# One stage of a delta-rule layer, rescheduled: mask product, convolution taps, key scaling, scores and output transposes

## The chip, the core and the metric

The kernel runs on one core of a Trainium2 chip. Its engines are TensorE (PE; its weight loads are a row of their own, PEld), VectorE (DVE), ScalarE (ACT), GpSimd (POOL) and SyncE (SP), which only issues DMAs here. The metric is the device time of one execution in microseconds (us); less is better.

## The reference, cut to what matters

One layer: a gated DeltaNet with eight heads beside a memory cross-attention, an output projection, and a SwiGLU feed-forward part. The change touches the DeltaNet alone. What it computes for each head:

```python
qkv = silu(causal_dwconv(qkv, conv_w))          # 4 taps along time
q = l2norm(q) * GDN_DK ** -0.5;  k = l2norm(k)
beta = sigmoid(b);  g = -exp(a_log) * softplus(a + dt_bias);  G = cumsum(g) in a chunk
decay = where(incl, exp(G_i - G_j), 0)
lower = where(strict, beta_i * (k_i . k_j) * decay, 0)
sol = triangular_solve(lower + I, [v * beta, k * beta * exp(G)])     # u, w
p = (q k^T) * decay;  qg = q * exp(G);  kg = k * exp(G_last - G)
# over chunks: v_new = u - w S;  o = qg S + p v_new;  S = S * exp(G_last) + kg^T v_new
y = rms_norm(o, out_norm) * silu(z)
```

The kernel uses chunks of 128 rows, which gives the same result.

## The kernel before

**Units and slots.** A head has eight chunks. Half a head (four chunks, `C4`, 128 x 512 elements) is a unit; there are 16 units, and the loop over `i` runs through 20 rounds. In round `i` four things go on side by side: the dense projection that makes the inputs of the heads (`dense`: 512-column matmuls of fp32r operands that are split into a high part `whi`, `uhi` and a low part `wlo`, `ulo`, three per product), the preparation of unit `i`, the inverse of unit `i-1` (`inverse`), and the recurrence over the four chunks of unit `i-2` (`scan`). Each round has 16 slots. In a slot stand one step of the inverse, one step of the scan, the steps that the table `STEPS` lists for that slot (function, lag in units), then perhaps one convolution tap (`TAPS`), then two groups of three dense matmuls (one group where a round has a single projection). An even round projects v and q of a head, an odd round k of the next head and z.

**The recurrence.** In the scan a chunk takes four slots: `r` (slots 0, 4, 8, 12), `vn` (1, 5, 9, 13), the new state `st` (2, 6, 10, 14), the output `po` (3, 7, 11, 15). TensorE makes a product into PSUM, VectorE turns it into the operand of the next product. The matmul `pc<-vn,kg` of slots 2, 6, 10 and 14 needs the `vn` of the slot before. The inverse goes on in the same way: even slots `pz`, then `zlev` on VectorE; odd slots `pT` and `pU`, then `T` and `U` on VectorE. Each of these takes the result of the slot before.

**What sets the order.** On TensorE the order is that of the code (`keep_in_program_order`, rounds 2 to 15). On the other engines a scheduler places the instructions; `tc.issue_after(x)` keeps an instruction behind `x`. `crit[0]` is the last VectorE instruction of inverse or scan so far; `tap()` puts its tap behind it. Each engine then works strictly through its own order.

**The steps that the change touches.** `conv_silu` leaves for each projected half two ScalarE copies from PSUM (`cb` L289, `cv` L290) and three taps on VectorE (L295, each reads `cb` and `cv` from SBUF); after the third, ScalarE applies Silu (L298). Halves end with slots 3, 7, 11 and 15. `k_norm` transposes the keys (`pk`), copies them to SBUF (`kh`, L435) and makes the inverse norm `rk` (squares on ScalarE, power on GpSimd, L85). `k_scale` multiplies `kh` by `rk` on VectorE (L443). `k_decay` makes `kg` (L449, two SBUF inputs) and on GpSimd `E` (L454, L455). `k_system` makes the matrix `at`, its fp16 high part `ah` (ScalarE, L485) and low part `al` (GpSimd, L486). `k_pairs` multiplies `ah` by a mask into `U` (L491, fp16, both inputs in SBUF); `k_first` transposes that `U` in slot 15 (`ptt`, `T` L499). `q_scores` makes `pqk`, `E` (L572) and `gr` (L573, GpSimd). `post` scales the output on GpSimd (L624 to L630), `post_y` transposes it (`pyt`) and multiplies it by z (L635), then stores it. Beside this GpSimd makes the low part of each weight tile, `wlo` (L93, 128 x 1024), and in odd rounds four differences of output weights, `wsum` (L650).

```python
    STEPS = {0: ((post, -3), (k_decay, 0)), 2: ((k_turn, 0),), 4: ((v_turn, -1),), 5: ((q_turn, -1),),
             7: ((k_system, 0),), 9: ((post_y, -3),), 10: ((k_norm, 1),), 11: ((q_scores, -1),), 13: ((k_pairs, 0),),
             15: ((k_scale, 1),)}
    TAPS = (0, 1, 2, 4, 5, 6, 8, 10, 11, 12, 14, 15)
```

Of the kernel before, what the change touches and what calls it, by code (L numbers as in the profile page):

```python
# [13 lines left out]
AF = mybir.ActivationFunctionType  # L14
ALU = mybir.AluOpType
AX = mybir.AxisListType

P = 128
# [36 lines left out]
def trunk_kernel(ctx: ExitStack, tc: tile.TileContext, a: dict, out: bass.AP):  # L55
    nc = tc.nc
# [122 lines left out]
    for tn in range(NT):  # L179
        hf, n = divmod(tn, 4)  # L180
# [22 lines left out]
        for q in range(2):  # L203
            pt = bank(("ms", "iv")[q], "pt")
            for j in range(4):
# [6 lines left out]
                                    in1=hi.bitcast(F32), op=ALU.subtract)  # L212
# [12 lines left out]
    C4 = 4  # L225
# [9 lines left out]
    mu = load_const(a["mu"], [P, P], F16, "mu_sb", up)  # L235
# [32 lines left out]
    def u4(tag, bufs, dt=F32, name=None):  # L268
        return hp.tile([P, C4, P], dt, tag=tag, name=name or tag, bufs=bufs)

    def flat(t):
        return t.rearrange("p n c -> p (n c)")
# [4 lines left out]
    def bc(col):  # L277
        return col.unsqueeze(2).broadcast_to([P, C4, P])
# [26 lines left out]
    def tap():  # L305

        while pending:
            with tc.issue_after(crit[0]) if crit[0] is not None else nullcontext():
                if next(pending[0], 0) is None:
                    return  # L310
            pending.pop(0)
# [3 lines left out]
            tap()  # L315

    crit = [None]

    def transposes(src, name):
        pt = bank("ms", name)  # L320
# [36 lines left out]
    st = [{} for _ in range(2 * H)]  # L357
# [23 lines left out]
    def tmp(name):  # L381
        return xp.tile(shp, F32, tag=name, name=name, bufs=1)

    beta, neg_eg, eg_last, eg_tot, gc = ct("beta"), ct("neg_eg"), ct("eg_last"), ct("eg_tot"), ct("gc")
# [35 lines left out]
                            in1=gc.rearrange("p h n -> p (h n)"), op=ALU.subtract)  # L420
# [10 lines left out]

    def k_norm(h, hf, hd, st):
        pk = transposes(hd["kT"][:, hf * C4:(hf + 1) * C4, :], "pk")
        kh = u4("kh", 2)
        nc.scalar.copy(flat(kh), pk)  # L435
        rk = small.tile([P, C4], F32, tag="rk", name="rk")
        rstd_into(rk, sumsq(pk), 1.0, C4)
        st.update(kh=kh, rk=rk)

    def k_scale(h, hf, hd, st):  # L440
        kh = st["kh"]
        with tc.issue_after(crit[0]) if crit[0] is not None else nullcontext():
            nc.vector.tensor_tensor(out=kh, in0=kh, in1=bc(st["rk"]), op=ALU.mult)  # L443

    def k_decay(h, hf, hd, st):

        n0 = hf * C4
        kg = u4("kg", 3)
        nc.vector.tensor_tensor(out=kg, in0=st["kh"], in1=bc(eg_last[:, h, n0:n0 + C4]), op=ALU.mult)  # L449
        gr = u4("gr", 3)  # L450
        st["gr_ins"] = nc.sync.dma_start(flat(gr), grow_d[h * NT + n0:h * NT + n0 + C4, :]
                                         .rearrange("n i -> (n i)").unsqueeze(0).broadcast_to([P, HF])).ins
        E = u4("E", 3)
        nc.gpsimd.tensor_tensor(out=E, in0=gr, in1=bc(gc[:, h, n0:n0 + C4]), op=ALU.subtract)  # L454
        nc.gpsimd.affine_select(out=E, in_=E, pattern=[[0, C4], [1, P]], compare_op=ALU.is_ge,  # L455
                                fill=-30000.0, base=0, channel_multiplier=-1)
        st.update(kg=kg, gr=gr, E=E)
# [30 lines left out]

    def k_pairs(h, hf, hd, st):
        U = st["U"] = u4("U", 2, F16)  # L490
        nc.vector.tensor_tensor(out=U, in0=st["ah"], in1=mu.unsqueeze(1).broadcast_to([P, C4, P]), op=ALU.mult)  # L491

    def k_first(h, hf, hd, st):
        U = st["U"]
# [166 lines left out]
    def stage(fn, u):  # L661
        if 0 <= u < 2 * H:
# [3 lines left out]

    SLOTS = 16
    STEPS = {0: ((post, -3), (k_decay, 0)), 2: ((k_turn, 0),), 4: ((v_turn, -1),), 5: ((q_turn, -1),),
             7: ((k_system, 0),), 9: ((post_y, -3),), 10: ((k_norm, 1),), 11: ((q_scores, -1),), 13: ((k_pairs, 0),),
             15: ((k_scale, 1),)}  # L670
    TAPS = (0, 1, 2, 4, 5, 6, 8, 10, 11, 12, 14, 15)
    stage(k_norm, 0)
    stage(k_scale, 0)

# [1 line left out]
    for hm in range(MH):  # L676
        whi, wlo = next_w()
        pk = bank("iv", "pkm")
# [785 lines left out]
```

## Time and profile before

| | us |
|---|---|
| median of three runs (1571.86 to 1574.34) | 1573.46 |
| the profiled execution | 1572.9 |
| its span, first to last instruction | 1570.7 |
| PE busy in the span | 1477.2 (94%) |
| DVE busy | 1087.2 (69%) |
| POOL busy | 820.7 (52%) |
| ACT busy | 671.3 (43%) |

The rounds of the recurrence fill the span from about 84 us to 659 us. An engine's busy time is the time in which an instruction of it runs; matmuls are pipelined and their ends are modelled, so neighbours overlap in the table. In the timeline a row in brackets tells how long the engine stood idle before it and what it waited for.

### The profile page before, as it was taken

To read this page: it belongs to the slowest core of one execution; us is meant where nothing else is said; L and a number is where in the kernel's file an instruction comes from. 1 tells how busy PE (TensorE), PEld (TensorE's weight loads), DVE (VectorE), ACT (ScalarE), POOL (GpSimd) and SP (SyncE) were. 2 spreads that over 40 slices of the span, in tenths; PEclk is the share of its full clock that TensorE was granted. 3 is DMA by queue.
4 is the path that set the end of the run, shared out by engine and by line. 5 is a ranking of instruction groups with operands and counts; after the bars stand their busy time and mean duration, and the time that the engine had idled before them with its cause. 6 is when DMAs were issued, how large, how long until landed. Compare 5 with 4: busy or idle time off the path is not lost. (4 is left out here: it accounts for less than half of the span.)

```text
span 1570.7 us, 22590 instructions
## 1 busy us (share of the span) xinstructions
PE 1477.2 (94%) x8237; PEld 1180.5 (75%) x8237; DVE 1087.2 (69%) x1667; ACT 671.3 (43%) x1433; POOL 820.7 (52%) x705
## 2 busy tenths in 40 slices
PE   7999999999999999999798789999999999999995
PEld 5777777777777777887586678877777887778784
DVE  7566767666676767667877887666666666585968
ACT  7464544544454544345446532222222222444352
POOL 3543536364645454302756656666666655544456
PEclk9999999999999999999999999999999999999998
DMA  5411212121212121217435222222222223973234
GB/s 199 155 55 42 78 58 95 47 95 62 76 60 88 62 74 42 68 55 234 169 101 180 81 74 97 97 99 97 98 91 101 101 89 137 318 261 100 88 95 167
DMA packets 77552, 168.12 MB, mean 107 GB/s; under 512 B 10433, under 2 KB 12929, under 8 KB 77442
## 3 DMA queue, kind: packets, MB, share of 16 engines
q1 hardware_dynamic: 76720, 165.58, 31.2%
q8 instruction: 64, 1.05, 0.3%
q10 hardware_dynamic: 722, 1.12, 0.2%
q14 instruction: 46, 0.38, 0.1%
HBM read 124.42 MB, written 42.24 MB: 106 GB/s over the span
## 5 line engine op out<-in xcount | busy, mean ns | idle before, releaser
L246 PE MATMUL pj<-uhi,whi 128*128 128x512 f32 x496 | 215.9, 435 | 0.0
L93 POOL TENSOR_TENSOR wlo<-raw,whi 128x1024 fp32r<-128x1024 f32 x61 | 157.4, 2580 | 74.5 <-ACT whi L92 74.4
L246 PE MATMUL pj<-uhi,wlo 128*128 128x512 f32 x496 | 195.9, 395 | 0.0
L246 PE MATMUL pj<-ulo,whi 128*128 128x512 f32 x496 | 194.0, 391 | 0.0
L1288 POOL TENSOR_TENSOR wlo<-ar,whi 128x512 fp32r<-128x512 f32 x75 | 105.9, 1413 | 99.6 <-ACT whi L1287 98.2
L295 DVE SCALAR_TENSOR_TENSOR cv<-cb,convw_sb,cv 128x512 f32<-128x512 f32 x144 | 127.4, 885 | 32.5 <-ACT cv L290 32.0
L903 PE MATMUL fo<-wlo,whi 128*128 128x512 f32 x308 | 122.4, 397 | 9.3 <-DVE wlo L1288 9.1
L1091 DVE TENSOR_TENSOR raw<-raw 128x512 f32<-128x512 f32 x86 | 104.7, 1218 | 25.6 <-POOL wlo L93 17.1
L904 PE MATMUL fo<-whi,wlo 128*128 128x512 f32 x308 | 120.1, 390 | 0.0
L92 ACT CAST whi<-raw 128x1024 fp32r<-128x1024 f32 x66 | 69.8, 1057 | 115.0 <-DVE raw L1053 59.1
L902 PE MATMUL fo<-whi 128*128 128x512 f32 x308 | 118.2, 391 | 0.7 <-DVE c L850 0.6
L1288 DVE TENSOR_TENSOR wlo<-B,whi 128x512 fp32r<-128x512 f32 x75 | 81.5, 1088 | 46.9 <-ACT whi L1287 46.5
L246 PEld LDWEIGHTS pj<-uhi,wlo 128*128 128x128 f32 x496 | 93.2, 188 | 21.2
L246 PEld LDWEIGHTS pj<-ulo,whi 128*128 128x128 f32 x496 | 94.3, 190 | 10.7
L246 PEld LDWEIGHTS pj<-uhi,whi 128*128 128x128 f32 x496 | 94.1, 190 | 10.8 <-issue 0.2
L1053 DVE TENSOR_TENSOR raw<-raw,gcols_sb 128x1024 f32<-128x1024 f32 x44 | 57.3, 1302 | 58.9 <-DMA raw<-in_w_ffn_in 58.5
L1287 ACT CAST whi<-ar 128x512 fp32r<-128x512 f32 x75 | 46.5, 621 | 113.2 <-POOL wlo L1288 77.2
L83 POOL TENSOR_SCALAR rs<-ss 128x1 f32<-128x1 f32 (+1 forms) x66 | 23.4, 354 | 111.7 <-ACT junk L329 86.1
L1074 POOL TENSOR_TENSOR qlo<-raw,qhi 128x1024 fp32r<-128x1024 f32 x21 | 55.8, 2655 | 48.1 <-ACT qhi L1073 46.6
L903 PE MATMUL acc<-wlo,whi 128*128 128x512 f32 x168 | 68.4, 407 | 13.2 <-DVE wlo L887 13.2
L903 PEld LDWEIGHTS fo<-wlo,whi 128*128 128x128 f32 x308 | 57.8, 188 | 29.0 <-DVE wlo L1288 17.6
L513 DVE TENSOR_TENSOR zlev<-pz,lvmask_sb 128x256 f16<-128x256 f32 x96 | 40.4, 421 | 50.0 <-PE pz L246 49.8
(409 smaller groups left out, 4288.2 us busy)
## 6 DMA issues: line engine op xcount, KB each, us to landing
raw<-in_w_ffn_in SPq DMA_DIRECT2D x44, 512.0 KB, 3.3
raw<-in_w_in SPq DMA_DIRECT2D x36, 512.0 KB, 3.3
ar<-g_S SPq DMA_DIRECT2D x44, 256.0 KB, 2.6
B<-in_w_ffn_out SPq DMA_DIRECT2D x42, 256.0 KB, 4.5
g_A<-g SPq DMA_DIRECT2D x33, 256.0 KB, 2.0
ar<-g_A SPq DMA_DIRECT2D x29, 256.0 KB, 3.6
wsum<-in_w_out SPq DMA_DIRECT2D x24, 256.0 KB, 4.3
T_d<-wsum SPq DMA_DIRECT2D x24, 256.0 KB, 2.0
```

The source lines that it names most:

```text
L92: nc.scalar.copy(hi, raw)
L93: (lo_eng or nc.gpsimd).tensor_tensor(out=lo, in0=raw, in1=hi.bitcast(F32), op=ALU.subtract)
L246: ins = nc.tensor.matmul(*args, **kw)
L295: nc.vector.scalar_tensor_tensor(out=cf, in0=cb[:, c0:c0 + HF], scalar=w[:, j:j + 1], in1=cf, op0=ALU.mult, op1=ALU.add)
L902: nc.tensor.matmul(acc[n], hi[:, 0, ts_], hi[:, 1], start=first, stop=False)
L903: nc.tensor.matmul(acc[n], hi[:, 0, ts_], lo[:, 1], start=False, stop=False)
L904: return nc.tensor.matmul(acc[n], lo[:, 0, ts_], hi[:, 1], start=False, stop=last)
L1053: nc.vector.tensor_tensor(out=raw, in0=raw, in1=gcol[:, 1, :].unsqueeze(2).broadcast_to([P, ND, P]), op=ALU.mult)
L1074: nc.gpsimd.tensor_tensor(out=lo, in0=src, in1=hi.bitcast(F32), op=ALU.subtract)
L1091: nc.vector.tensor_tensor(out=o, in0=x, in1=y, op=op)
L1287: nc.scalar.copy(hi[:, i], src)
L1288: last_lo[i] = eng.tensor_tensor(out=lo[:, i], in0=src, in1=hi[:, i].bitcast(F32), op=ALU.subtract).ins
```

## The change

Six moves, all in the rounds of the recurrence:

- `k_pairs` (the mask product L491) goes from slot 13 to slot 11 and is now held behind `crit[0]`.
- The taps of each half come a slot later where they followed at once: `TAPS` loses 0, 11 and 12 and gains 3, 9 and 13.
- `k_norm` no longer copies the keys; `k_scale` writes `kh` from PSUM with four ScalarE activations whose scale is `rk`, in slot 13 instead of 15. The VectorE product L443 and the ScalarE copy L435 are gone.
- `k_decay` holds `kg` behind `crit[0]`.
- `q_scores` goes from slot 11 to 12.
- `post_y` goes from slot 9 to 15.

```diff
-            with tc.issue_after(crit[0]) if crit[0] is not None else nullcontext():
+            with behind():
@@
+    def behind():
+
+        return tc.issue_after(crit[0]) if crit[0] is not None else nullcontext()
@@ k_norm
-        kh = u4("kh", 2)
-        nc.scalar.copy(flat(kh), pk)
         rk = small.tile([P, C4], F32, tag="rk", name="rk")
         rstd_into(rk, sumsq(pk), 1.0, C4)
-        st.update(kh=kh, rk=rk)
+        st.update(pk=pk, rk=rk)
@@ k_scale
-        kh = st["kh"]
-        with tc.issue_after(crit[0]) if crit[0] is not None else nullcontext():
-            nc.vector.tensor_tensor(out=kh, in0=kh, in1=bc(st["rk"]), op=ALU.mult)
+        kh = st["kh"] = u4("kh", 2)
+        for n in range(C4):
+            nc.scalar.activation(kh[:, n, :], st["pk"][:, n * P:(n + 1) * P], AF.Copy, scale=st["rk"][:, n:n + 1])
@@ k_decay
-        nc.vector.tensor_tensor(out=kg, in0=st["kh"], in1=bc(eg_last[:, h, n0:n0 + C4]), op=ALU.mult)
+        with behind():
+            nc.vector.tensor_tensor(out=kg, in0=st["kh"], in1=bc(eg_last[:, h, n0:n0 + C4]), op=ALU.mult)
@@ k_pairs
-        nc.vector.tensor_tensor(out=U, in0=st["ah"], in1=mu.unsqueeze(1).broadcast_to([P, C4, P]), op=ALU.mult)
+        with behind():
+            nc.vector.tensor_tensor(out=U, in0=st["ah"], in1=mu.unsqueeze(1).broadcast_to([P, C4, P]), op=ALU.mult)
@@
-             7: ((k_system, 0),), 9: ((post_y, -3),), 10: ((k_norm, 1),), 11: ((q_scores, -1),), 13: ((k_pairs, 0),),
-             15: ((k_scale, 1),)}
-    TAPS = (0, 1, 2, 4, 5, 6, 8, 10, 11, 12, 14, 15)
+             7: ((k_system, 0),), 10: ((k_norm, 1),), 11: ((k_pairs, 0),), 12: ((q_scores, -1),),
+             13: ((k_scale, 1),), 15: ((post_y, -3),)}
+    TAPS = (1, 2, 3, 4, 5, 6, 8, 9, 10, 13, 14, 15)
```

Where the scheduler puts things is seen in the order of the built programs. VectorE, slots 8 to 11 of a round before (`r` and `vn` belong to the scan, `T`, `U` from PSUM and `zlev` to the inverse, `U<-ah,mu_sb` is the mask product, `cv` are taps):

```order
L588 SCALAR_TENSOR_TENSOR r<-pc,neg_eg,vt 128x128
L491 TENSOR_TENSOR U<-ah,mu_sb 128x512
L526 TENSOR_TENSOR T<-pT,T 128x8x32
L528 TENSOR_TENSOR U<-pU,U 128x8x32
L295 SCALAR_TENSOR_TENSOR cv<-cb,convw_sb,cv 128x512
L593 TENSOR_SCALAR vn<-pc,beta 128x128
L635 SCALAR_TENSOR_TENSOR zs<-pyt,onorm_sb,zs 128x512
L513 TENSOR_TENSOR zlev_433<-pz,lvmask_sb 128x4x64
L602 SCALAR_TENSOR_TENSOR st<-st,eg_tot,pc 128x128
L295 SCALAR_TENSOR_TENSOR cv<-cb,convw_sb,cv 128x512
```

The mask product stood there although its slot is 13, since nothing held it back. The same place now:

```order
L592 SCALAR_TENSOR_TENSOR r<-pc,neg_eg,vt 128x128
L530 TENSOR_TENSOR T<-pT,T 128x8x32
L532 TENSOR_TENSOR U<-pU,U 128x8x32
L295 SCALAR_TENSOR_TENSOR cv<-cb,convw_sb,cv 128x512
L597 TENSOR_SCALAR vn<-pc,beta 128x128
L295 SCALAR_TENSOR_TENSOR cv<-cb,convw_sb,cv 128x512
L517 TENSOR_TENSOR zlev_433<-pz,lvmask_sb 128x4x64
L606 SCALAR_TENSOR_TENSOR st<-st,eg_tot,pc 128x128
L295 SCALAR_TENSOR_TENSOR cv<-cb,convw_sb,cv 128x512
L530 TENSOR_TENSOR T<-pT,T 128x4x64
L532 TENSOR_TENSOR U<-pU,U 128x4x64
L495 TENSOR_TENSOR U<-ah,mu_sb 128x512
```

The mask product has gone behind the `T` and `U` of slot 11; one tap still stands between `U` and `vn` of slot 9.

VectorE, slots 0 to 3 of an odd round before:

```order
L588 SCALAR_TENSOR_TENSOR r<-pc,neg_eg,vt 128x128
L295 SCALAR_TENSOR_TENSOR cv<-cb,convw_sb,cv 128x512
L526 TENSOR_TENSOR T<-pT,T 128x128x2
L528 TENSOR_TENSOR U<-pU,U 128x128x2
L593 TENSOR_SCALAR vn<-pc,beta 128x128
L295 SCALAR_TENSOR_TENSOR cv<-cb,convw_sb,cv 128x512
L513 TENSOR_TENSOR zlev_425<-pz,lvmask_sb 128x64x4
L602 SCALAR_TENSOR_TENSOR st<-st,eg_tot,pc 128x128
L295 SCALAR_TENSOR_TENSOR cv<-cb,convw_sb,cv 128x512
L526 TENSOR_TENSOR T<-pT,T 128x64x4
L528 TENSOR_TENSOR U<-pU,U 128x64x4
```

and now:

```order
L592 SCALAR_TENSOR_TENSOR r<-pc,neg_eg,vt 128x128
L452 TENSOR_TENSOR kg<-kh,eg_last 128x512
L530 TENSOR_TENSOR T<-pT,T 128x128x2
L532 TENSOR_TENSOR U<-pU,U 128x128x2
L597 TENSOR_SCALAR vn<-pc,beta 128x128
L295 SCALAR_TENSOR_TENSOR cv<-cb,convw_sb,cv 128x512
L517 TENSOR_TENSOR zlev_425<-pz,lvmask_sb 128x64x4
L606 SCALAR_TENSOR_TENSOR st<-st,eg_tot,pc 128x128
L295 SCALAR_TENSOR_TENSOR cv<-cb,convw_sb,cv 128x512
L530 TENSOR_TENSOR T<-pT,T 128x64x4
L532 TENSOR_TENSOR U<-pU,U 128x64x4
L295 SCALAR_TENSOR_TENSOR cv<-cb,convw_sb,cv 128x512
```

The first tap is gone from the place ahead of `T` and `U`, `kg` has come in its stead, and a tap now follows the `U` of slot 3.

TensorE, slot 15, now (`ptt` is the transpose of the masked `U`, `po` the output of the last chunk, `pyt` the transposes of the output):

```order
L250 MATMUL ptt<-ident_sb,U 128x128
L246 MATMUL po<-st,gr 128x128
L246 MATMUL po<-vn,E 128x128
L250 MATMUL pyt<-ident_sb,os 128x128 x4
L246 MATMUL pj<-uhi_128,whi 128x512
```

Before, the four `pyt` stood in slot 9, and `pj` followed on `po` here.

## Rows read from the trace of the kernel before

**Rows 1.** Windows: stretch, length, busy (instructions) of PE PEld DVE ACT POOL, clock, DMA.

```profile
150.00:590.00 440.00, 422.09 (x3131) 335.43 (x3130) 295.86 (x600) 213.18 (x553) 228.98 (x257) 1.00 0.21 72
```

**Rows 2.** Waits of PE from 95 to 650 us: total us, times, longest us.

```profile
PE pc L246 <- DVE vn L593: 19.4, 20, 1.2
PE pz L246 <- DVE T L526: 2.7, 3, 1.8
PE pz L246 <- ACT T L499: 1.6, 1, 1.6
```

**Rows 3.** Timeline of PE: start us, duration us, instruction, [idle before <- releaser]; slot 10.

```profile
153.28 0.49 PE L246 MATMUL pc<-vn,kg 128*128 128x128 f32 x2 [1.21 <-DVE vn L593]
...
593.26 0.49 PE L246 MATMUL pc<-vn,kg 128*128 128x128 f32 x2 [1.18 <-DVE vn L593]
```

**Rows 4.** Timeline of PE, odd round: slots 1, 2, 5, 6, 9, 10.

```profile
315.01 0.29 PE L246 MATMUL pT<-zlev,U 128*128 128x64 f16 x4
...
316.94 0.29 PE L246 MATMUL pz<-T,ah 128*128 128x64 f16 x4
...
323.64 0.29 PE L246 MATMUL pT<-zlev,U 128*128 128x64 f16 x4
...
326.88 0.49 PE L246 MATMUL pc<-vn,kg 128*128 128x128 f32 x2 [0.58 <-DVE vn L593]
...
333.47 0.29 PE L246 MATMUL pT<-zlev,U 128*128 128x64 f16 x4
...
335.85 0.29 PE L246 MATMUL pz<-T,ah 128*128 128x64 f16 x4
337.31 0.49 PE L246 MATMUL pc<-vn,kg 128*128 128x128 f32 x2 [1.16 <-DVE vn L593]
```

**Rows 5.** Timeline of DVE, the same odd round: slots 5, 8 and 9.

```profile
325.48 0.75 DVE L295 SCALAR_TENSOR_TENSOR cv<-cb,convw_sb,cv 128x512 f32<-128x512 f32 x1 [1.09 <-ACT cv L290]
...
326.49 0.34 DVE L593 TENSOR_SCALAR vn<-pc,beta 128x128 f32<-128x128 f32 x1
...
333.21 2.21 DVE L491 TENSOR_TENSOR U<-ah,mu_sb 128x512 f16<-128x512 f16 x1 [0.55 <-ACT ah L485]
...
335.67 0.41 DVE L528 TENSOR_TENSOR U<-pU,U 128x256 f16<-128x256 f32 x1
336.00 0.98 DVE L295 SCALAR_TENSOR_TENSOR cv<-cb,convw_sb,cv 128x512 f32<-128x512 f32 x1
336.91 0.34 DVE L593 TENSOR_SCALAR vn<-pc,beta 128x128 f32<-128x128 f32 x1
```

**Rows 6.** Timeline of POOL, the same odd round.

```profile
320.55 0.64 POOL L455 TENSOR_SCALAR_AFFINE_SELECT E<-E 128x512 f32<-128x512 f32 x1
321.15 2.39 POOL L93 TENSOR_TENSOR wlo<-raw,whi 128x1024 fp32r<-128x1024 f32 x1
...
332.74 2.40 POOL L93 TENSOR_TENSOR wlo<-raw,whi 128x1024 fp32r<-128x1024 f32 x1 [0.37 <-ACT whi L92]
335.10 1.35 POOL L486 TENSOR_TENSOR al<-at,ah 128x512 f16<-128x512 f32 x1
336.40 4.77 POOL L650 TENSOR_TENSOR wsum<-wsum 128x512 f32<-128x512 f32 x3
```

**Rows 7.** Timeline of ACT, the same odd round, slot 5.

```profile
324.69 0.69 ACT L290 ACTIVATE cv<-pj,convw_sb 128x512 f32<-128x512 f32 x1
```

**Rows 8.** Timeline of DVE, round 15, slot 3.

```profile
611.45 2.88 DVE L295 SCALAR_TENSOR_TENSOR cv<-cb,convw_sb,cv 128x512 f32<-128x512 f32 x1
```

**Rows 9.** Timeline of POOL, round 15.

```profile
611.41 2.37 POOL L93 TENSOR_TENSOR wlo<-raw,whi 128x1024 fp32r<-128x1024 f32 x1
```

**Rows 10.** Timeline of POOL, round 0.

```profile
93.47 1.03 POOL L85 TENSOR_TENSOR rk<-rs,mhalf 128x4 f32<-128x4 f32 x1
```

**Rows 11.** Timeline of DVE, round 0, three taps.

```profile
95.87 2.32 DVE L295 SCALAR_TENSOR_TENSOR cv<-cb,convw_sb,cv 128x512 f32<-128x512 f32 x3
```

**Rows 12.** Timeline of PE, start of round 1.

```profile
99.37 0.28 PE L246 MATMUL pz<-T,ah 128*128 128x64 f16 x4 [1.64 <-ACT T L499]
```

## The prediction

> **What bounds the kernel now.** I read three views in this order. First the windows, for the rounds of the recurrence: PE is busy 422 of 440 us at a granted clock of 1.00 (the 2.4 GHz level), DVE 296, ACT 213, POOL 229 [rows 1]. So TensorE is the bound and the most that any rescheduling can win there is its idle time, about 4%. Second, who ends that idle time: almost all of it is the matmul `pc<-vn,kg`, which waits for VectorE's `vn`, 19.4 us in 20 waits; the matmul `pz` waits 2.7 us for `T` (3 times) and once 1.6 us for the ScalarE copy of `T` [rows 2]. Third, where the waits lie. 13 of the 20 stand in slot 10 of rounds 2 to 14, from 153.28 to 593.26, 1.2 us each [rows 3]; six stand in slot 6 of the odd rounds 3 to 13, 0.58 us each, like the one at 326.88 [rows 4]; one is in slot 2 of round 15. Two of the `pz` waits, 0.9 us together, are slot 10 of rounds 1 and 2, the third (1.8 us) is in round 15.
>
> Why is `vn` late in slot 10? VectorE's own rows tell: the mask product starts at 333.21 and takes 2.21 us, then follow `T`, `U`, a tap and `vn`, which ends at 337.25; the matmul starts 0.06 us later [rows 4, 5]. The mask product is a small fp16 operation; its length is a wait. GpSimd's `wlo` runs from 332.74 to 335.14, and the product ends 0.28 us after that [rows 5, 6]. The tap behind it (0.98 us) ends at 336.98, which is 0.53 us after the end of `al` at 336.45 [rows 5, 6]. The clearest case is round 15: a tap issued at 611.45 takes 2.88 us and ends 0.55 us after a `wlo` that ends at 613.78 [rows 8, 9]. So a VectorE instruction with two SBUF inputs waits for the running GpSimd instruction to end and then takes its 0.28 us (mask) or 0.55 us (tap).
>
> **The change, part by part.** *Mask product.* Moving it behind `T` and `U` of slot 11 removes it from slot 9. Nothing needs it before the `ptt` of slot 15. In slot 11 it may again wait for a GpSimd instruction, in odd rounds for one of the `wsum`, 4.77 us for three, so 1.6 us [rows 6]; behind it stands `e`, which first needs the products of slot 12. A slot lasts at least some 1.9 us (315.01 to 316.94 [rows 4]), so this wait is covered; without that cover it would cost up to 1.6 us in six rounds.
>
> What is late next in slot 9? Not the mask product, but the tap that still stands between `U` and `vn`. `T` and `U` take 0.41 us each after `pT` at 333.47, so that tap is issued before 335.1, in the middle of `wlo`. By the rule above it ends at 335.14 + 0.55 = 335.69, and `vn`, 0.34 us of which 0.08 overlap, at 335.95; the matmul follows at 336.00 instead of 337.31, 1.31 us earlier. Of this, 0.45 us are not won but moved: from `pT` to the next `pz` slot 9 takes 2.38 us with the four `pyt`, slot 1 takes 1.93 us without them [rows 4], and these transposes now run in slot 15. Gain: 1.31 - 0.45 = 0.86 us, in 13 rounds 11.2 us. Some 0.3 us of idle time stays in each slot 10. The bounds are 0 per round (the tap also waits for `al`) and 1.16 (nothing waits).
>
> The Trainium skill has a rule for this, in "SBUF — State Buffer", section "Who interferes with whom": the read interface that VectorE needs for a second SBUF input is shared with GpSimd, as an exclusive lock that whoever issues first keeps for the whole instruction. It speaks against counting the whole idle time as won: a reader who takes the mask product for the only cause would write 13 x 1.16 = 15.1 us, by this rule it is the 11.2 us above. The trace agrees (2.88 us for a tap behind a `wlo`).
>
> *Output transposes to slot 15.* `pyt` stands behind `po` there, so the chain that starts at `po` (ScalarE's squares, GpSimd's `post` and `E`, ScalarE's exponentials and copies, the tap of slot 4) keeps its times while TensorE gets to slot 6 0.45 us later. Today the tap is issued when ScalarE's copy ends (324.69 + 0.69 = 325.38) and `vn` ends at 326.83 [rows 5, 7]. So the idle 0.58 us becomes 0.13: 6 x 0.45 = 2.7 us. Bounds: 0 and 0.58 per round. VectorE's product of `pyt` lies in slot 15 ahead of `zlev`, where a whole dense group covers it, and the store that SP issues behind it holds up only loads whose data is due slots later.
>
> *Taps a slot on.* In odd rounds slot 0 loses its tap ahead of `T` (nothing waited there), and a tap comes behind `U` of slot 3. The `pT` of slot 3 lies midway between 315.01 and 323.64, at 319.3, now 0.45 later; with `T` and `U` the tap is issued at about 320.6. GpSimd's select runs from 320.55 to 321.19, so the tap ends at 321.74 and `wlo` (321.15) is held 0.55 us [rows 4, 6]. `zlev` of slot 4 comes after that anyway: no cost, with 0.5 us to spare. In slots 9 and 10 the moved tap waits for `al` and, in odd rounds, for a `wsum`; `zlev` of slot 10 then has about 0.5 us left.
>
> *Keys on ScalarE.* Four activations of 128 columns replace a 512-column copy. The nearest row is the 512-column `cv`, 0.69 us [rows 7]; a quarter of it each is 0.7 us in all, a whole one each 2.8 us; I take 0.8. ScalarE is 48% busy [rows 1], and `kh` is due only in slot 2 of the next round, so steady rounds pay nothing. VectorE loses a product of the kind of `kg`. *Scores* move 0.8 us of TensorE work by a slot, with no net effect.
>
> *The ends of the stretch.* At the start of round 1 TensorE waits 1.64 us for ScalarE's `T` [rows 12]. That waits for three taps at 95.87 [rows 11]. Now the key activations wait for `rk` at 94.50 [rows 10], and behind them stand a Silu and the copies that the taps need: 94.50 + 0.8 + three instructions of up to 0.69 give 97.3, 1.4 us later; a part is hidden, so -1.3 us (0 to -2). The 0.9 us of rounds 1 and 2 go. Round 15 waits 0.6 + 1.8 us today; the tap behind `wlo` moves to slot 3 and delays `zlev` instead of `T`: I take half of it, +1.1 us (0 to 2.4).
>
> **How it adds up.** 11.2 + 2.7 + 0.9 + 1.1 - 1.3 = 14.6 us. The span falls from 1570.7 to 1556.1 us, the profiled execution from 1572.9 to 1558.3. That execution lies 0.6 us below the median of 1573.46, from which the same sum gives 1558.9; I say **1559**.
>
> **The rivals.** *All waits go* (0.12): the tap of slot 9 comes out ahead of `wlo`, and the start costs nothing. Another 13 x 0.3 + 6 x 0.13 + 1.3 = 6 us: 1553. Against it: the tap cannot be issued before 332.74.
>
> *The tap of slot 3 meets `wlo`* (0.14): if it is issued 0.5 us later than I reckon, it ends at 321.15 + 2.39 + 0.55 = 324.09, `zlev` at 324.4, while `pT` of slot 5 is due at 324.09; 0.4 to 1 us in six rounds, 1561 to 1565. (The Trainium skill, "SBUF — State Buffer", "Who interferes with whom", has this outcome whenever `wlo` issues first, at the same price.)
>
> *ScalarE's queue takes the gain* (0.07): the key activations wait for `rk`, which in odd rounds follows three `wsum`; if the copies of the projection behind them come later than a slot group allows, TensorE waits a microsecond or more in each round, and the time lands within 0.2% of today, 1570 to 1576. For it: ScalarE works strictly in order. Against: several slots lie between.
>
> *GpSimd keeps the port* (0.05), the slower side: the tap of slot 9 is served only when GpSimd's queue runs dry, not between two instructions that stand back to back. It would then end at 336.40 + 4.77 + 0.55 = 341.7 in the six odd rounds with `wsum`, 4.7 us after today's matmul; with the 0.45 us each of `pyt` some 34 us of loss against 3.4 us of other gains: 1604. It decides at the end of `wlo`; today's mask product got through there, although `al` stood behind.
>
> **How the numbers follow.** The forecast, 1556 to 1562, has 0.62. Against 0.2% of the time, about what a measurement of this kernel can tell from no change: faster 0.62 + 0.12 + 0.14 = 0.88, same 0.07, slower 0.05. The range of 1552 to 1567 takes in the first three cases and the bounds of the ends.
>
> **What would show it.** Right: `pc<-vn,kg` waits about 0.3 us in slot 10 and 0.1 us in slot 6; the mask product takes under 2 us and sits in slot 11; the tap ahead of `vn` in slot 9 takes about 1.2 us and ends 0.55 us after `wlo`. Wrong: a tap in slot 3 of odd rounds of over 2 us, new waits of `pT` for `zlev` in slots 5 or 11, ScalarE idle ahead of the key activations with the copies of the projection queued behind, or a slot 10 that still waits over 1 us.

## The result, and the profile after

The changed kernel takes 1555.07 us (median of 4 runs, 1551.72 to 1557.43), the kernel before 1572.66 us (4 runs beside it): ratio 0.9897, 95% interval 0.9866 to 0.9929. Forecast: 1559, range 1552 to 1567. Its profiled execution took 1557.43 us, its span 1555.3 us.

Windows of after, the stretch of [rows 1] (stretch, length, busy time and instructions of PE, PEld, DVE, ACT, POOL, clock, DMA share, GB/s):

```profile
150.00:590.00 440.00, 435.13 (x3234) 346.20 (x3232) 285.86 (x607) 226.67 (x614) 233.95 (x259) 1.00 0.22 74
```

TensorE is busy 435 of 440 us instead of 422, at the same clock; VectorE has lost 10 us, ScalarE gained 13.5. The waits of PE from 95 to 650 us, against [rows 2]:

```profile
PE pc L246 <- DVE vn L597: 5.2, 15, 1.0
PE pz L246 <- ACT T L503: 1.6, 1, 1.6
PE pz L246 <- DVE T L530: 1.6, 2, 1.3
PE pT L246 <- DVE zlev L517: 0.5, 1, 0.5
```

The wait for `vn` fell from 19.4 to 5.2 us. The timeline of PE says where the rest stands: the first and last slot 10, the one in the middle of the stretch, and two slots 6 of odd rounds (3 and 7), against [rows 3, 4]:

```profile
150.48 0.38 PE L246 MATMUL pc<-vn,kg 128*128 128x128 f32 x1 [0.30 <-DVE vn L597]
...
328.52 0.38 PE L246 MATMUL pc<-vn,kg 128*128 128x128 f32 x1 [0.30 <-DVE vn L597]
...
576.03 0.38 PE L246 MATMUL pc<-vn,kg 128*128 128x128 f32 x1 [0.30 <-DVE vn L597]
```

```profile
177.82 0.38 PE L246 MATMUL pc<-vn,kg 128*128 128x128 f32 x1 [0.96 <-DVE vn L597]
...
319.44 0.36 PE L246 MATMUL pc<-vn,kg 128*128 128x128 f32 x1
```

Slot 10 idles 0.30 us in all 13 rounds. Slot 6 idles 0.96 us in round 3, the first round with a `post` (no output turns stand yet in slot 15 of the round before), and not at all in rounds 5 to 13. VectorE and GpSimd in slot 9 of the same round, against [rows 5, 6]:

```profile
326.65 0.41 DVE L532 TENSOR_TENSOR U<-pU,U 128x256 f16<-128x256 f32 x1
326.99 1.22 DVE L295 SCALAR_TENSOR_TENSOR cv<-cb,convw_sb,cv 128x512 f32<-128x512 f32 x1
328.13 0.34 DVE L597 TENSOR_SCALAR vn<-pc,beta 128x128 f32<-128x128 f32 x1
...
332.06 0.85 DVE L495 TENSOR_TENSOR U<-ah,mu_sb 128x512 f16<-128x512 f16 x1
```

```profile
325.27 2.39 POOL L93 TENSOR_TENSOR wlo<-raw,whi 128x1024 fp32r<-128x1024 f32 x1 [0.37 <-ACT whi L92]
327.62 1.61 POOL L489 TENSOR_TENSOR al<-at,ah 128x512 f16<-128x512 f32 x1
```

The mask product stands in slot 11 and takes 0.85 us here, where it ends 0.28 us after a `wsum`, as it ended 0.28 us after `wlo` before the change. In slot 11 of an even round only a small power runs on GpSimd, and it takes 0.42 us:

```profile
295.97 0.42 DVE L495 TENSOR_TENSOR U<-ah,mu_sb 128x512 f16<-128x512 f16 x1
```

```profile
295.46 1.03 POOL L85 TENSOR_TENSOR rk<-rs,mhalf 128x4 f32<-128x4 f32 x1
```

So most of the 2.21 us was its wait and not its work. The tap in front of `vn` ends at 328.21, 0.55 us after `wlo` (327.66), although `al` stands right behind: it waits for one GpSimd instruction, not for the queue.

**A measure finer than the time.** Executions of one kernel fall into two groups (the kernel before in the first set below: six from 1562.71 to 1565.53 us, nine from 1572.51 to 1579.83), further apart than most edits are worth. The recurrence does not: from the start of its first `vn` to that of its last it takes 509.94 us in the first profile of the changed kernel and 509.99 us in the second. So the edits are judged by this stretch, and by what lies between the last `vn` and the first `acc` of the stage behind. All in us, from the timelines:

| kernel | first vn | last vn | stretch | last vn to first acc |
|---|---|---|---|---|
| before | 133.07 | 658.91 | 525.84 | 56.73 |
| changed | 131.56 | 641.50 | 509.94 | 57.51 |
| changed, again | 135.93 | 645.92 | 509.99 | 57.45 |
| before + mask product moved | 130.44 | 639.40 | 508.96 | 56.79 |
| changed, output turns in slot 9 | 133.30 | 643.06 | 509.76 | 57.52 |
| changed, keys on VectorE | 132.79 | 642.70 | 509.91 | 57.49 |
| changed, old taps | 130.54 | 645.82 | 515.28 | 57.50 |
| changed, taps 9, 10, 11 | 130.62 | 634.22 | 503.60 | 57.53 |
| changed, scores in slot 11 | 134.96 | 645.16 | 510.20 | 56.79 |
| both of these | 133.14 | 638.21 | 505.07 | 56.78 |
| taps 9, 10, 11, last scores in 11 | 131.60 | 635.19 | 503.59 | 57.49 |
| the same, other taps in round 15 | 133.33 | 636.92 | 503.59 | 57.51 |
| changed, mask product back | 133.32 | 660.08 | 526.76 | 57.53 |
| turns in slot 9, `kg` early | 132.49 | 661.81 | 529.32 | 57.49 |

### The profile page after: what moved, and what is told of

Its sections match the earlier page's. It is cut to its first block, busy times and chain, and to the rows that moved or that the text cites. A ratio compares the mean times of both kernels' runs of the same rounds, so it can differ in the third digit from the quotient of the medians.

```text
span 1555.3 us, 22654 instructions
## 1 busy us (share of the span) xinstructions
PE 1477.7 (95%) x8237; PEld 1180.3 (76%) x8237; DVE 1067.9 (69%) x1651; ACT 680.4 (44%) x1481; POOL 822.4 (53%) x705
## 5 line engine op out<-in xcount | busy, mean ns | idle before, releaser
L295 DVE SCALAR_TENSOR_TENSOR cv<-cb,convw_sb,cv 128x512 f32<-128x512 f32 x144 | 132.6, 921 | 24.0 <-ACT cv L290 23.3
L1095 DVE TENSOR_TENSOR raw<-raw 128x512 f32<-128x512 f32 x86 | 100.3, 1167 | 23.7 <-POOL wlo L93 13.7
L1057 DVE TENSOR_TENSOR raw<-raw,gcols_sb 128x1024 f32<-128x1024 f32 x44 | 64.1, 1457 | 57.9 <-DMA raw<-in_w_ffn_in 57.5
L530 DVE TENSOR_TENSOR T<-pT,T 128x256 f16<-128x256 f32 x96 | 40.6, 423 | 59.5 <-PE pT L246 58.8
```

The source lines that it names most:

```text
L295: nc.vector.scalar_tensor_tensor(out=cf, in0=cb[:, c0:c0 + HF], scalar=w[:, j:j + 1], in1=cf, op0=ALU.mult, op1=ALU.add)
L1057: nc.vector.tensor_tensor(out=raw, in0=raw, in1=gcol[:, 1, :].unsqueeze(2).broadcast_to([P, ND, P]), op=ALU.mult)
L1095: nc.vector.tensor_tensor(out=o, in0=x, in1=y, op=op)
```

## The experiments

**The changed kernel again.**

> The changed kernel once more, beside its variants on one chip. Theory: as in its first profile, 16 to 18 us under the kernel before, with 0.30 us of idle time ahead of pc<-vn,kg in slot 10 of rounds 2 to 14 and none in slot 6 except in round 3. The first profile lay 1.55 us ahead of the kernel before at the product pab, at 45 us, where no changed instruction stands yet, and gave back about 2 us after the recurrence. If both are chance of one execution, this profile shows other values there while the recurrence from the first to the last pz again takes 15.8 us less than before; if the change causes them (by the order in which tiles are placed), they return with the same sign.

1558.15 us (10 runs), ratio 0.9914 (0.9883 to 0.9944). The recurrence repeats to 0.05 us and the loss of 0.75 us behind it stays; `pab` starts 0.53 us later than before instead of 1.55 us earlier. So the 1.55 us were chance of one execution and the 0.75 us belong to the change.

**The mask product alone.** The kernel before with

```diff
-        nc.vector.tensor_tensor(out=U, in0=st["ah"], in1=mu.unsqueeze(1).broadcast_to([P, C4, P]), op=ALU.mult)
+        with behind():
+            nc.vector.tensor_tensor(out=U, in0=st["ah"], in1=mu.unsqueeze(1).broadcast_to([P, C4, P]), op=ALU.mult)
...
-             7: ((k_system, 0),), 9: ((post_y, -3),), 10: ((k_norm, 1),), 11: ((q_scores, -1),), 13: ((k_pairs, 0),),
+             7: ((k_system, 0),), 9: ((post_y, -3),), 10: ((k_norm, 1),), 11: ((k_pairs, 0), (q_scores, -1)),
```

> The kernel before, with the mask product alone moved behind U of slot 11; output turns stay in slot 9, the taps and keys as before. My theory (the mask product's wait for wlo is what makes vn late in slot 10; behind it only the tap is late, at 335.69 + 0.3): with the four pyt still in slot 9 TensorE is busy until vn is there, so slot 10 loses its 1.16 us of idle time in all 13 rounds, 15.1 us, while slot 6 keeps 0.58 us in six odd rounds. 15 to 16 us under the kernel before, so as fast as the whole change or up to 1 us slower. Rival (the other edits are needed as well, because the mask product of slot 11 with the old taps of slots 10 and 11 makes e or zlev late): new waits of pe or pv in slots 12 and 13, 3 to 10 us under the kernel before.

1553.62 us, ratio 0.9885 (0.9842 to 0.9929). Waits of PE from 95 to 650 us:

```profile
PE pc L246 <- DVE vn L598: 4.4, 8, 0.6
PE pz L246 <- DVE T L531: 1.8, 1, 1.8
PE pz L246 <- ACT T L504: 1.6, 1, 1.6
```

The eight waits are slot 6 of six rounds (0.58 each), slot 10 of round 2 (0.30) and one of round 15; slot 10 of rounds 3 to 14 waits no more. The stretch is 16.9 us shorter, against 15.9 for the whole change; 15 to 16 were expected: in rounds 3 to 14 the time from the last `pz` to `pc` fell from 1.37 to 0.07 us or less, more than the 1.16 us of idle time. The rival falls.

**The mask product back.** The changed kernel with this one edit undone:

```diff
-        with behind():
-            nc.vector.tensor_tensor(out=U, in0=st["ah"], in1=mu.unsqueeze(1).broadcast_to([P, C4, P]), op=ALU.mult)
+        nc.vector.tensor_tensor(out=U, in0=st["ah"], in1=mu.unsqueeze(1).broadcast_to([P, C4, P]), op=ALU.mult)
...
-             7: ((k_system, 0),), 10: ((k_norm, 1),), 11: ((k_pairs, 0),), 12: ((q_scores, -1),),
-             13: ((k_scale, 1),), 15: ((post_y, -3),)}
+             7: ((k_system, 0),), 10: ((k_norm, 1),), 12: ((q_scores, -1),),
+             13: ((k_pairs, 0), (k_scale, 1)), 15: ((post_y, -3),)}
```

> The changed kernel with the mask product alone put back ahead of T in slot 9 (where it waits for wlo); all other edits stay. Theory (the mask product is what the change earns, the rest only moves waits): slot 10 of rounds 2 to 14 idles 1.16 us as before plus the 0.45 us of the output turns that no longer stand in slot 9, 1.6 us; 13 x 1.31 = 17 us more than the changed kernel, the stretch from the first to the last vn about 527 us, as long as before the change (525.8) or a little longer, and the time within 0.3% of the kernel before. Rival (the other edits have a gain of their own, by the taps and VectorE's relief): at least 3 us under the kernel before.

1573.64 us, ratio 1.0005 (0.9979 to 1.0032); the stretch is 526.76 us. VectorE in slots 8 and 9 of round 7, and the matmuls of slot 10:

```profile
333.99 2.21 DVE L494 TENSOR_TENSOR U<-ah,mu_sb 128x512 f16<-128x512 f16 x1 [0.55 <-ACT ah L488]
336.12 0.41 DVE L529 TENSOR_TENSOR T<-pT,T 128x256 f16<-128x256 f32 x1
```

```profile
336.58 0.28 PE L246 MATMUL pz<-T,ah 128*128 128x64 f16 x4 [0.24 <-DVE T L529]
338.07 0.49 PE L246 MATMUL pc<-vn,kg 128*128 128x128 f32 x2 [1.21 <-DVE vn L596]
```

The 2.21 us are back, and so is the wait (0.24 + 1.21 us; 1.6 were expected). Moving the mask product is thus enough for the gain, and the gain is not had without it.

**The output turns back in slot 9.** The changed kernel with

```diff
-             7: ((k_system, 0),), 10: ((k_norm, 1),), 11: ((k_pairs, 0),), 12: ((q_scores, -1),),
-             13: ((k_scale, 1),), 15: ((post_y, -3),)}
+             7: ((k_system, 0),), 9: ((post_y, -3),), 10: ((k_norm, 1),), 11: ((k_pairs, 0),), 12: ((q_scores, -1),),
+             13: ((k_scale, 1),)}
```

> The changed kernel with the output turns pyt back in slot 9. My theory of the prediction (they cover 0.45 us in the slot in which they stand, and it is their move that filled slot 6): slot 10 loses its 0.30 us in 13 rounds (-3.9 us), slot 6 of the odd rounds gets 0.45 us back in six rounds (+2.7 us), so 1.2 us under the changed kernel. Rival (slot 6 was filled by the taps, which now stand one slot later and pass GpSimd's queue in another order): slot 6 stays without idle time, 3.9 us under the changed kernel. Either way the move of the output turns does not earn time; if it does, this kernel is slower than the changed one by 1 us or more.

Ratio 0.9897 (0.9852 to 0.9941); the stretch is 0.2 us shorter. Slot 10 idles no more from round 3 on (0.30 us in round 2, which has no turns), and slot 6 idles 0.96 us in all six odd rounds, not 0.45. Neither theory had that. With the next run there are four combinations; idle time in us in slot 6 of odd rounds from round 5 on (the upper left is the kernel before with the mask product moved, where `kg` too stands early and the keys are made as before):

| | turns in slot 9 | turns in slot 15 |
|---|---|---|
| old taps | 0.58 | 0.17 |
| new taps | 0.96 | 0 |

**The old taps in the changed kernel.**

```diff
-    TAPS = (1, 2, 3, 4, 5, 6, 8, 9, 10, 13, 14, 15)
+    TAPS = (0, 1, 2, 4, 5, 6, 8, 10, 11, 12, 14, 15)
```

> The changed kernel with the tap slots of before (0, 1, 2, 4, 5, 6, 8, 10, 11, 12, 14, 15). It tells apart what filled slot 6. The runs so far: 0.58 us of idle time in slot 6 of odd rounds before and with the mask product moved alone; 0.96 with the changed kernel when the output turns are back in slot 9; none in the changed kernel from round 5 on. Theory 1 (plain cover, the prediction's): the turns in slot 15 cover 0.45 us whatever the taps do, so slot 6 idles 0.13 us, slot 10 0.30 us. Theory 2 (a race for the port between VectorE's kg and taps of slots 0 to 3 and GpSimd's post): a tap that is issued again in slot 0, behind kg, blocks one of the small products of post for up to 0.5 us, and the slack of 0.14 us that vn has in slot 6 of the changed kernel turns into 0.3 to 0.5 us of idle time. Round 1 tells the rest: if the wait of pT for zlev (0.55 us at 119.33) comes from the tap of slot 10, it goes.

One execution, 1561.03 us. Slot 6 of round 7:

```profile
318.77 0.38 PE L246 MATMUL pc<-vn,kg 128*128 128x128 f32 x1 [0.17 <-DVE vn L597]
```

0.58 - 0.17 = 0.41 us: with these taps the turns cover what the prediction said (0.45). GpSimd's products of `post` take in that round what they took with the mask product moved alone, so theory 1 holds there. Nearly 4 of the 5.3 us by which the stretch is longer arise in round 15, where waits of 1.74, 0.31 and 0.99 us stand close together and the granted clock is 0.50 from 597 to 603 us. The wait of `pT` for `zlev` at 119.33 goes, so it comes from the places of the taps.

**`kg` early.** What made slot 6 worse with the new taps? The kernel with the turns back in slot 9, and

```diff
-        with behind():
-            nc.vector.tensor_tensor(out=kg, in0=st["kh"], in1=bc(eg_last[:, h, n0:n0 + C4]), op=ALU.mult)
+        nc.vector.tensor_tensor(out=kg, in0=st["kh"], in1=bc(eg_last[:, h, n0:n0 + C4]), op=ALU.mult)
```

> The changed kernel with the output turns in slot 9 (whose slot 6 idled 0.96 us in the odd rounds) and, beside that, kg issued as early as before the change, between the taps of slots 14 and 15 instead of behind r of slot 0. It asks what made slot 6 worse, from 0.58 to 0.96 us. Theory A (kg): in slot 0 it runs from 308.61 to 309.29 in the kernel with the turns back, and GpSimd's power of post, which takes 1.01 us elsewhere, takes 1.41 there; without kg the power takes 1.0 us and slot 6 idles about 0.55 us. Theory B (the tap of slot 3, under which GpSimd's select takes 1.09 instead of 0.64 us): slot 6 stays at 0.96 us or falls by less than 0.1.

Slot 6 idles 0.08 us, where theory A had 0.55. GpSimd's power of `post`, first with `kg` in slot 0 (the kernel with the turns back), then with `kg` early:

```profile
308.75 1.41 POOL L85 TENSOR_TENSOR sc<-rs,mhalf 128x4 f32<-128x4 f32 x1
```

```profile
314.72 1.01 POOL L85 TENSOR_TENSOR sc<-rs,mhalf 128x4 f32<-128x4 f32 x1
```

In the first, VectorE's `kg` runs from 308.61 to 309.29, issued 0.14 us ahead of the power; in the changed kernel `kg` is issued at 307.42, 0.27 us behind the power (307.15), which takes 1.01 us. Two later steps of the same chain on GpSimd account for the rest. The select of slot 3, first with `kg` in slot 0, then with `kg` early:

```profile
314.95 1.09 POOL L458 TENSOR_SCALAR_AFFINE_SELECT E<-E 128x512 f32<-128x512 f32 x1
```

```profile
320.52 0.64 POOL L457 TENSOR_SCALAR_AFFINE_SELECT E<-E 128x512 f32<-128x512 f32 x1
```

And the product `sc<-sc,rq`, first in the kernel with the mask product moved alone (old taps), then with `kg` early (new taps):

```profile
306.26 0.69 POOL L633 TENSOR_TENSOR sc<-sc,rq 128x4 f32<-128x4 f32 x1
```

```profile
315.82 0.20 POOL L631 TENSOR_TENSOR sc<-sc,rq 128x4 f32<-128x4 f32 x1
```

Late by the power's 0.40 us, the select comes 0.25 us behind the tap of slot 3 (issued at 314.70) and takes 0.45 us longer; with `kg` early it comes 0.15 us ahead of that tap (320.67). So theory A's `kg` is the cause, and theory B's tap is half of its price. The tap that the change takes out of slot 0 was issued 0.12 us ahead of `sc<-sc,rq` in the kernel with the old taps and held it 0.49 us. The idle times follow: 0.58 - 0.49 = 0.09 with `kg` early (0.08 measured), and 0.09 + 0.40 + 0.45 = 0.94 with `kg` ahead of the power (0.96). Who issues first in slot 0 decides, and the 0.45 us that the turns take in slot 15 turn the order round; in round 3 of the changed kernel, which has no turns in the slot 15 before it, `kg` is first and the power takes 1.42 us. But the run lost 2.5 us in each of six rounds elsewhere, in the slot of `pv`:

```profile
344.61 0.69 DVE L451 TENSOR_TENSOR kg<-kh,eg_last 128x512 f32<-128x512 f32 x1 [4.23 <-ACT kh L445]
```

```profile
345.95 0.40 PE L246 MATMUL pv<-U,e 128*128 128x128 f16 x4 [2.50 <-DVE e L539]
```

Without its place behind `r`, `kg` comes ahead of `e` on VectorE in these rounds, and waits for the keys, which wait on ScalarE for `rk`, which stands behind GpSimd's `wsum`. It is the chain of the prediction's rival of ScalarE's queue, `rk` behind `wsum`, but what comes late is `kg` and with it `e`, not the copies of the projection. Behind the wait the granted clock falls in five of the six rounds (0.72 over 346 to 352 us; 1.00 over 420.5 to 426.5 in the sixth). The place behind `r`, a part of the change, is what keeps this away.

**The keys on VectorE.** `k_norm` and `k_scale` as before the change, all else changed.

> The changed kernel with the keys made as before: ScalarE copies them out of PSUM, VectorE multiplies them in place. My theory: steady rounds pay nothing either way, since kh is due only in slot 2 of the next round; at the start of round 1, where TensorE waited 1.62 us for T with ScalarE's activations, the same wait as before the change, the wait stays, since it did not grow when the activations came: 0 us, within 1 us of the changed kernel. Rival A (the activations held back the start by as much as something else won there): 1 to 1.5 us faster. Rival B (VectorE's relief is a part of the gain, above all in slots 14 and 15): new waits for vn in slot 14 or for kg in slot 2, 1 to 5 us slower.

Ratio 0.9897 (0.9859 to 0.9934), stretch 509.91 us, the same waits of `vn`, and 1.67 us at the start of round 1 against 1.62 and 2.23 in the two profiles of the changed kernel. Which engine scales the keys makes no difference that these runs show.

**The taps of slots 8, 9, 10 in slots 9, 10, 11.**

```diff
-    TAPS = (1, 2, 3, 4, 5, 6, 8, 9, 10, 13, 14, 15)
+    TAPS = (1, 2, 3, 4, 5, 6, 9, 10, 11, 13, 14, 15)
```

> The changed kernel with the three taps of slots 8, 9 and 10 one slot later (9, 10, 11), so that no tap stands between U and vn in slot 9. Theory (the 0.30 us left in slot 10 are the tap that waits for wlo): vn follows U and ends some 0.8 us earlier, the 0.30 us go in all 13 rounds. A wait takes 0.12 us more from TensorE than its idle time shows (from the last pz to pc 0.49 us with 0.30 idle, 0.07 us where nothing waits), so the stretch from the first to the last vn is 13 x 0.42 = 5.5 us shorter than the 509.9 of the changed kernel: 504.4. Rival A (al and the wsum take the port first and the taps of slots 9 to 11 are late for zlev of slot 10 or e of slot 12): new waits of pT in slot 11 or pe in slot 13, 0.5 us and more in odd rounds, a gain under 3 us. Rival B (vn was late for pc itself, not for the tap): 0.30 us stay.

One execution, 1551.49 us. VectorE in slot 9 of round 7, then TensorE's slot 10:

```profile
323.29 0.41 DVE L532 TENSOR_TENSOR U<-pU,U 128x256 f16<-128x256 f32 x1
323.62 0.34 DVE L597 TENSOR_SCALAR vn<-pc,beta 128x128 f32<-128x128 f32 x1
323.88 0.96 DVE L295 SCALAR_TENSOR_TENSOR cv<-cb,convw_sb,cv 128x512 f32<-128x512 f32 x1
```

```profile
324.57 0.29 PE L246 MATMUL pz<-T,ah 128*128 128x64 f16 x4
324.69 0.36 PE L246 MATMUL pc<-vn,kg 128*128 128x128 f32 x1
```

`vn` follows `U`, and slot 10 idles in no round. The stretch is 6.3 us shorter than with the change, 0.8 more than expected: from the last `pz` to `pc` TensorE takes 0.49 us with the wait and 0.03 us without, not 0.07, which is 0.5 of the 0.8. Both rivals fall.

**The scores.** First in slot 11 again:

```diff
-             7: ((k_system, 0),), 10: ((k_norm, 1),), 11: ((k_pairs, 0),), 12: ((q_scores, -1),),
+             7: ((k_system, 0),), 10: ((k_norm, 1),), 11: ((k_pairs, 0), (q_scores, -1)),
```

> The changed kernel with the scores back in slot 11. In all profiles with the scores in slot 12 the stage behind the recurrence gives time back: against the kernel before, the first psc lies 1.83 us less early than the last pz, the first acc 0.76 us less early; with the mask product moved alone both lie as early as the last pz. Theory (in the last round but one the last output turns and the memory's first products hang on the slot of the scores): the first acc is 0.7 to 0.8 us earlier against the last pz than in the changed kernel, the recurrence unchanged (0 to 0.1 us). Rival (another edit does it, the output turns in slot 15): the 0.76 us stay.

One execution, 1558.92 us. The last column of the table falls to 56.79, as before the change: the 0.75 us come from moving the scores. The stretch is 0.2 to 0.3 us longer, where 0 to 0.1 was expected.

Then this edit and the taps in 9, 10, 11 together:

> The changed kernel with the taps in slots 9, 10 and 11 and the scores in slot 11. If both theories hold, they add: 5.5 + 0.76 = 6.3 us under the changed kernel, which makes it 2 to 4 us faster than the mask product moved alone, about 1549 us, 1.4% under the kernel before. Rival (VectorE's slot 11, now mask product, tap and the product of the scores ahead of e, is too full): a new wait of pe or pv in slots 12 and 13 of the odd rounds, at the most what slot 11's wait for a wsum costs, 0.4 to 1.6 us in six rounds, and the kernel is no faster than the changed one.

1552.36 us, ratio 0.9872 (0.9832 to 0.9911). Behind the recurrence the 0.75 us are back, but the stretch is 1.5 us longer than with the scores in slot 12. The two do not simply add; the net is a loss of 0.7 us. The rival's waits of `pe` and `pv` do not show; about 0.2 us go in each of the six odd rounds.

Then the taps in 9, 10, 11, the scores in slot 12, and

```diff
+    LAST = {**STEPS, 11: ((k_pairs, 0), (q_scores, -1)), 12: ()}
...
-            for fn, lag in STEPS.get(s, ()):
+            for fn, lag in (LAST if i == 2 * H else STEPS).get(s, ()):
```

> The changed kernel with the taps in slots 9, 10 and 11, and the scores in slot 12 but for the last round in which they occur (round 16), where they stand in slot 11. The runs so far: taps 9, 10, 11 alone shorten the stretch from the first to the last vn from 509.9 to 503.6 us; with the scores in slot 11 of all rounds it is 505.1, but the 0.8 us behind the recurrence come back. Theory: the two are separate, the scores earn 0.2 us in each odd round by standing in slot 12 and cost 0.8 us only through the round in which the last output turns hang on them. So 503.6 us for the recurrence and a first acc that lies as far ahead as the last pz: 22.2 us under the kernel before at the first acc, less what the start of the execution adds or takes. Rival: the 0.8 us hang on the scores of round 15 too, and the first acc lies 0.8 us less far ahead than the last pz.

1547.96 us, ratio 0.9837 (0.9809 to 0.9866). The stretch is as expected, and behind it stand 57.49 us, the rival's number. So the 0.75 us do not hang on the slot of round 16; that they hang on round 15 is not shown. What the traces show is where they lie: in all ten profiles that have the scores of the earlier rounds in slot 12, TensorE stands idle 0.53 to 0.56 us ahead of the last `pyt` (at 651.01 in the changed kernel), for nothing that the profile names, and in none of the four with slot 11.

**Round 15.** The last kernel, and

```diff
-            if s in TAPS:
+            if s in ((1, 2, 5) if i == 2 * H - 1 else TAPS):
```

> The kernel of the run with the scores' last round in slot 11, and beside it the three taps of round 15 in slots 1, 2 and 5 instead of 1, 2 and 3. In round 15 a pz waits 1.28 us for T, which stands behind a tap that was issued in slot 3 while wlo ran. Theory: in slot 5 the tap comes behind the end of wlo, T of slot 3 or 5 is on time, the 1.28 us go (1.4 us in all), and no other wait of round 15 grows. Rival (the tap in slot 5 meets the next GpSimd instruction, or kg and the product of gr are what makes round 15 late): a wait of 0.5 us or more takes the place, and the stretch is as long.

1548.65 us, ratio 0.9831 (0.9801 to 0.9860), the same stretch to 0.01 us. I had moved the wrong tap. Timeline of DVE, POOL and PE in round 15:

```profile
589.44 0.33 DVE L606 SCALAR_TENSOR_TENSOR st<-st,eg_tot,pc 128x128 f32<-128x128 f32 x1
589.70 2.88 DVE L295 SCALAR_TENSOR_TENSOR cv<-cb,convw_sb,cv 128x512 f32<-128x512 f32 x1
592.50 0.41 DVE L530 TENSOR_TENSOR T<-pT,T 128x256 f16<-128x256 f32 x1
```

```profile
589.66 2.37 POOL L93 TENSOR_TENSOR wlo<-raw,whi 128x1024 fp32r<-128x1024 f32 x1
```

```profile
592.97 0.22 PE L246 MATMUL pz<-T,ah 128*128 128x64 f16 x2 [1.27 <-DVE T L530]
```

The tap that meets `wlo` comes behind `st`: it is that of slot 2, issued 0.04 us after `wlo`, and again it ends 0.55 us after it (592.58 and 592.03).

The two last kernels beat both kernels that this is about: their intervals (0.9809 to 0.9866, 0.9801 to 0.9860) lie under that of the changed kernel run again (0.9883 to 0.9944), and their stretch is 6.4 us shorter. What they have over it that shows in the traces is the place of three taps.

## Why the prediction was right, point by point

**Slot 10** (forecast 13 x 0.86 = 11.2 us). From the last `pz` to `pc` TensorE took 1.37 us and takes 0.49: 13 x 0.88 = 11.4 us. The 0.30 us that remain, and their cause, were forecast and are shown by the run without a tap in that place. The rule of the Trainium skill, "SBUF — State Buffer", "Who interferes with whom", that whoever issues first keeps the shared interface for its whole instruction, agrees with the tap behind `wlo` (2.88 us) and with GpSimd's power behind `kg` (1.41 for 1.01 us). It does not agree with VectorE behind a small power: the mask product of an even round begins 0.51 us into one of 1.03 us and ends inside it, after its 0.42 us. So the prediction's sentence that a VectorE instruction with two SBUF inputs waits for the running GpSimd instruction to end is shown for `wlo`, `al` and `wsum`, and is too wide for the 128x4 power.

**Slot 6** (2.7 us from 0.45 us of cover). Measured: five rounds by 0.75 and one worse by 0.38, 3.4 us. The cover is right with the old taps (0.41). With the new taps the step failed: it took GpSimd's times in slots 0 to 3 as given. The tap that leaves slot 0 frees one of its products (0.49 us), which alone leaves only 0.08 us of idle time; `kg` in slot 0 costs 0.40 + 0.45 us where it is issued ahead of the power, as in round 3; and from round 5 on the turns in slot 15 put it behind the power. None of this was in the term, so that it came out near 2.7 us is luck.

**Rounds 1 and 2** (0.9 us). Those two waits are gone, but a `pT` now waits 0.55 us for `zlev` in slot 11 of round 1, one of the signs the prediction listed against itself.

**Start of round 1** (-1.3 us). Nothing in the first profile: 1.62 us, against 1.64 [rows 12]. In the eleven profiles with the keys on ScalarE the wait is 1.47 to 2.35 us, 1.88 on average, against 1.56 to 1.67 in the three with the keys on VectorE; so at the most some 0.3 of the 1.3 us, inside the spread. The step counted what ScalarE gets and not what VectorE loses in the same chain. ScalarE and VectorE of the changed kernel, against [rows 10, 11]:

```profile
91.51 0.37 ACT L445 ACTIVATE kh<-pk,rk 128x128 f32<-128x128 f32 x1 [2.75 <-POOL rk L85]
91.78 0.62 ACT L298 ACTIVATE cv<-cv 128x512 f32<-128x512 f32 x1
92.30 0.87 ACT L445 ACTIVATE kh<-pk,rk 128x128 f32<-128x128 f32 x3
...
93.51 0.72 ACT L290 ACTIVATE cv<-pj,convw_sb 128x512 f32<-128x512 f32 x1
```

```profile
94.27 2.33 DVE L295 SCALAR_TENSOR_TENSOR cv<-cb,convw_sb,cv 128x512 f32<-128x512 f32 x3 [2.88 <-ACT cv L290]
```

The four activations take 0.37 + 0.87 = 1.2 us (0.8 were reckoned). But the taps now start 0.04 us after ScalarE's `cv`, where before the products for `kh` and `kg`, 0.69 us each, stood between (94.61 to 95.87).

**Round 15** (+1.1 us). Waits of 0.6 + 1.8 us became 0.29, 0.31 and 1.28 us, so +0.5. The step that the tap behind `wlo` moves to slot 3 was wrong; it is still the tap of slot 2.

**Scores** ("no net effect"). 0.75 us lost behind the recurrence, which the sum did not look at. In the recurrence slot 12 is 0.3 us better than slot 11 with the changed taps and 1.5 us better with the taps a slot on.

**The sum.** 11.2 + 2.7 + 0.9 + 1.1 - 1.3 = 14.6 us were forecast. The recurrence gained 15.9, the start nothing, and 0.75 us went behind it: about 15.1. The first profile's span fell by 15.4 us. The main term is right by its mechanism; the smaller ones miss by 0.5 to 1.3 us, and that their errors cancel is luck. That the first median lies 4 us under the forecast and the second (1558.15) 1 us is the spread of the executions.

What the prediction did not see is that the mask product alone does better than the whole: 16.9 us and no loss behind, against 15.9 and 0.75. (The stretch shows this; the times alone, with intervals that overlap, do not.) By its own steps moving the turns takes 13 x 0.45 us from slot 10 and gives 6 x 0.45 to slot 6; that difference, 3.2 us, stood in its sum unremarked. The runs make it smaller with the new taps (0.2 us), since there the turns take 0.96 us of idle time from slot 6, more than their own length: the cover, and the order of `kg` and the power.

## What to carry to other kernels

Look for a small operation with a long duration ahead of a critical one: its length may be another engine's instruction, and moving it behind the critical one can be worth more than all the rest of a plan. Then ask what stands there next; here a tap in the same place was worth another 6.3 us of the recurrence. Work that covers a wait is a budget: moving it from the slot that waits in thirteen rounds to cover one that waits in six won nothing (509.94 against 509.76 us), and each part of a bundle is worth undoing alone.

## What the runs showed of the hardware

**A wait costs more than its idle time.** The last matmul ahead of it counts as busy to its modelled end: 0.30 us of idle time cost 0.49 - 0.03 = 0.46 us in slot 10.

**A wait at the start can cost clock too.** TensorE waits 1.62 us for `T` ahead of round 1 in one profile of the changed kernel, 2.23 us in the other (until 100.75). Windows of 3 us, first of the one, then of the other (PEclk is the third number from the end):

```profile
97.00:100.00 3.00, 2.21 (x20) 1.72 (x20) 1.29 (x3) 2.76 (x5) 2.53 (x2) 1.00 0.02 5
100.00:103.00 3.00, 3.00 (x20) 2.25 (x18) 2.96 (x5) 1.07 (x2) 1.42 (x1) 1.00 0.18 40
```

```profile
100.00:103.00 3.00, 2.25 (x9) 1.87 (x9) 1.03 (x2) 2.72 (x5) 2.56 (x2) 0.59 0.03 5
103.00:106.00 3.00, 3.00 (x24) 2.05 (x24) 1.58 (x4) 0.00 (x0) 1.41 (x1) 0.84 0.17 48
```

The clock stayed at the 2.4 GHz level in the first; in the second it fell to the 1.2 GHz level for some microseconds, and the first `vn` came 35.2 us after the first `pz` instead of 33.8. The length of the wait alone does not decide it: in the run with `kg` early TensorE waited 2.35 us at this place, and the clock stayed at 1.00.

**Where the spread comes from.** At least a part of it is a wait of the stage behind, from 950 to 1300 us: 6.8 us in the kernel before, 5.6 in the changed one. With the taps in 9, 10, 11 and round 16's scores in slot 11 TensorE was busy 350.00 of 350 us there in the profiled execution, which had the shortest span of all, 1538.3 us; it is the only one of the fourteen profiles without this wait, and from the first `acc` to the end it took 845.6 us, the others 851.8 to 858.5. Its window, and the waits of PE in that stretch of before and of after:

```profile
950.00:1300.00 350.00, 350.00 (x1532) 287.29 (x1531) 222.73 (x271) 98.89 (x129) 217.87 (x109) 1.00 0.30 105
```

```profile
PE sc L137 <- POOL qlo L1074: 6.8, 7, 2.0
```

```profile
PE sc L137 <- POOL qlo L1078: 5.6, 5, 2.4
```
